# Where tiles start in SBUF: small tiles first, chunks and weight buffers 32 bytes further apart

## The chip, the core and the metric

The kernel runs on one core of a Trainium2 chip. Its engines are TensorE (PE: matmuls, and PEld: the load of the stationary operand), VectorE (DVE), ScalarE (ACT), GpSimd (POOL) and SyncE (SP, which issues most DMAs). They work from SBUF, a memory of 128 partitions; TensorE writes its sums into PSUM. The metric is the device time of one execution in microseconds (us); lower is better.

## What is computed

The reference is an encoder of two layers on 512 positions with 1024 features, all in float32. Each layer has a mixer and an MLP, with RMS norms in front and a last norm behind.

```python
for layer in range(DEPTH):                       # DEPTH = 2
    h = rms_norm(x, norm_mix[layer])
    if layer % N_MIXERS == 0:
        y = stick_breaking_attention(h, sb_w_qkv[ia], sb_w_o[ia])   # 16 heads of 64
    else:
        y = rglru_block(h, rg_w_in[ib], ..., rg_w_o[ib])            # gated linear recurrence, width 1024
    x = x + y
    h = rms_norm(x, norm_mlp[layer])
    x = x + squared_relu_mlp(h, mlp_w1[layer], mlp_w2[layer])       # relu(h @ w1)**2 @ w2, width 4096
return rms_norm(x, norm_final)
```

## The kernel before

**Split products.** Every large product is done with operands in two parts, a rounded high part (`float32r`) and the rest: `xgh` and `xgl` for the normed activations, `wh` and `wl` for the weights. `three` (lines 217 to 221) makes one product of a 128x128 block of weights with 512 columns of activations out of three matmuls: `wh` with the high activations (L219), `wl` with the high ones (L220), `wh` with the low ones (L221). The first operand of a matmul after the sum is the stationary one, which is loaded by an instruction of its own; the other, the moving one, is streamed through.

**Layout of activations.** `xgh`, `xgl`, `bh` and `bl` are tiles of 128 partitions by 8 chunks by 512 columns of 4 bytes: a chunk is 2048 bytes in each partition. `xgh` and `xgl` hold the normed input of a product; `bh` and `bl` the input of an output projection or, in the MLP, a part of the activations behind relu and square.

**Weights.** A slab of 1024x128 weights is fetched into a `raw` buffer, ScalarE copies it rounded into `wh`, and VectorE subtracts to get `wl` (`slab_parts`, `slab`, `operand`, `weights_high`). The pool `wpool` has four buffers of each; in the recurrent mixer a second pool, `wmore`, has two more. A slab is 4096 bytes in each partition.

**The MLP** uses a scheme of seven products of half-size blocks in place of eight. Its up projection (`up`, L965) has matmuls of 256 moving columns: slices of `xgh` and `xgl`, or of sums of them (`s41`, `low`, and a chunk of `bh` and `bl`), against slices of `wh` and `wl`. Its down projection (`times`, L1060) has the activations as the stationary operand (`bh` and `bl` for one half, `sh` and `sl` for the other) and 512 columns of `wh` or `wl` as the moving one. The value product of the attention (L475 to L477) has `xgh` and `xgl` as the stationary operand and 256 columns of weights as the moving one.

**Order and pools.** TensorE's order is the program's; the other engines are scheduled by the framework, in parts by hand. Pools take SBUF one behind the other in the order in which they are made, and a pool lays out its tiles by their names in the order in which they first occur; each tile is rounded up to 32 bytes. Tiles of 4 to 32 bytes (`eps_t`, the eight `lam_` tiles, `rt`, `rc`, `rp`, `rn`, `rr`) stand between the large ones. Pools that are closed leave their place to the next: the attention's tiles, the MLP's blocks and the recurrent mixer's tiles use the same bytes one after the other.

Of the kernel before, what the change touches and what calls it, by code (L numbers as in the profile page):

```python
# [61 lines left out]
def hybrid_encoder(  # L62
# [23 lines left out]
    nc = tc.nc  # L86
    V, A, G, PE = nc.vector, nc.scalar, nc.gpsimd, nc.tensor

    const = ctx.enter_context(tc.tile_pool(name="const", bufs=1))
    wpool = ctx.enter_context(tc.tile_pool(name="wpool", bufs=4))  # L90
    work = ctx.enter_context(tc.tile_pool(name="work", bufs=2))
# [22 lines left out]
    V.memset(ones, 1.0)  # L114
    ident = const.tile([P, P], F32, tag="ident", name="ident")
    make_identity(nc, ident)
    eps_t = const.tile([P, 1], F32, tag="eps", name="eps_t")
    V.memset(eps_t, EPS)

    xgh = const.tile([P, C, S], F32R, tag="xgh", name="xgh")  # L120
    xgl = const.tile([P, C, S], F32R, tag="xgl", name="xgl")
    bh = const.tile([P, C, S], F32R, tag="bh", name="bh")
    bl = const.tile([P, C, S], F32R, tag="bl", name="bl")

# [16 lines left out]
    class Squares:  # L141
# [21 lines left out]
        def inv_squares(self, ps):  # L163

            for t in range(S // P):
                PE.matmul(
                    ps[:, t : t + 1], self.acc[:, t * P : (t + 1) * P], ones[:, 0:1],
                    start=True, stop=True,
                )
            n = S // P  # L170
            rr = work.tile([P, 2 * n], F32, tag="rr", name="rr", bufs=1)
            V.tensor_scalar(rr[:, :n], ps[:, :n], 1.0 / D, EPS, ALU.mult, ALU.add)
            V.reciprocal(rr[:, :n], rr[:, :n])
            V.tensor_scalar(rr[:, n:], rr[:, :n], -1.0, None, ALU.mult)
            return rr


    def slab_parts(src, cuts):

        raw = wpool.tile([P, C, P], F32, tag="raw", name="raw", bufs=3)  # L180
        wh = wpool.tile([P, C, P], F32R, tag="wh", name="wh")
        wl = wpool.tile([P, C, P], F32R, tag="wl", name="wl")

        def fetch(i, queue=nc.sync):
            k = slice(*cuts[i : i + 2])
            queue.dma_start(out=raw[:, k, :], in_=src[:, k, :])

        def part(i, high=A.copy):
            k = slice(*cuts[i : i + 2])
            if high:  # L190
                high(wh[:, k, :], raw[:, k, :])
            if high == V.tensor_copy:
                return
            V.tensor_tensor(wl[:, k, :], raw[:, k, :], f(wh[:, k, :]), ALU.subtract)

        return wh, wl, fetch, part
# [5 lines left out]
    def slab(src, cut=1, ks=range(C)):  # L202
        raws = rawpools[next(loads) % len(rawpools)]
        raw = raws.tile([P, C, P], F32, tag="raw", name="raw", bufs=3 if raws is wpool else 1)
        k = slice(ks.start, ks.stop)
        nc.sync.dma_start(out=raw[:, k, :], in_=src[:, k, :])
        pool = wpools[next(slabs) % len(wpools)]
        wh = pool.tile([P, C, P], F32R, tag="wh", name="wh")
        wl = pool.tile([P, C, P], F32R, tag="wl", name="wl")
        for i in range(cut):  # L210
            k = slice(ks.start + i * len(ks) // cut, ks.start + (i + 1) * len(ks) // cut)
            A.copy(wh[:, k, :], raw[:, k, :])  # L212
            with tc.issue_after(behind[0]) if behind[0] else nullcontext():
                V.tensor_tensor(wl[:, k, :], raw[:, k, :], f(wh[:, k, :]), ALU.subtract)  # L214
        return wh, wl
# [15 lines left out]
    def beside(ws, ah, al, pss, at, ks=range(C)):  # L231
# [9 lines left out]


    lams = {
        n: const.tile([P, C], F32, tag=f"lam_{n}", name=n)
        for n in ("ab", "pp", "den", "s1", "s2", "pl", "c8", "c4")
    }
    c8, c4 = lams["c8"], lams["c4"]
# [42 lines left out]
    with ExitStack() as actx:  # L290
# [8 lines left out]
            fill=1.0, base=0, channel_multiplier=1,  # L299
        )  # L300

        scans = []
        for i in range(3):
            sc = sp.tile([P, S + 1], F32, tag=f"scan{i}", name=f"scan{i}")
            G.memset(sc[:, S : S + 1], 1.0)
            scans.append(sc)

        lasts = []
        for i in range(2):
            both = []  # L310
            for nm in ("h", "l"):
                t = sp.tile([P, 2 * P], F32R, tag=f"last{nm}{i}", name=f"last{nm}{i}")
                G.memset(f(t[:, :P]), 0.0)
                both.append(t)
            lasts.append(both)

        q, kh, kl, v, w = {}, {}, {}, {}, {}
        norm = {}
# [74 lines left out]
        others = {getattr(mybir.EngineType, e) for e in ("Activation", "DVE", "Pool", "SP")}  # L393
        with tc.manual_schedule(engines=others):
            A.dma_start(out=colt, in_=cols)
            A.activation(work.tile([P, 1], F32, tag="rt", name="early"), eps_t, AF.Sqrt)
            for j in range(2):
                parts[j][2](1, A)
            for c in range(C):
                nc.sync.dma_start(out=xcs[c], in_=xT[:, c, :])  # L400
                if c in (0, 3, 5):
                    for j in range(2):
                        parts[j][2]((c + 1) // 2)
            for j in range(2, 6):
                for i in range(2):
                    parts[j][2](i)

            parts[0][3](0, V.tensor_copy)
            for kind, c in START:
                if kind == "x":  # L410
                    halves("mix0", c, xcs[c])
                elif (kind, c) == ("q", 0):
                    parts[0][3](c, None)
                elif kind != "s":
                    parts["qknm".index(kind)][3](c)
                else:
                    A.activation(sqs[c], xcs[c], AF.Square)
                    if c:
                        V.tensor_tensor(sums, sums, sqs[c], ALU.add)

            for k in range(C):
                for n, (low, y) in enumerate(((0, xgh), (0, xgl), (1, xgh))):
                    for i in range(2):
                        PE.matmul(
                            first[i], parts[i][low][:, k, :], y[:, k, :], start=k == n == 0,
                            stop=k == C - 1 and n == 2,
                        )
            first_halves(*first)

        def inverse():  # L430

            pc = bank("z")
            for t in range(NB):
                PE.matmul(
                    pc[:, t : t + 1], sums[:, t * P : (t + 1) * P], ones[:, 0:1],
                    start=True, stop=True,
                )
            rc, rp, rn = (work.tile([P, NB], F32, tag=n, name=n, bufs=1) for n in ("rc", "rp", "rn"))
            diag = work.tile([P, S], F32, tag="sq", name="diag")
            with tc.high_priority():  # L440
                norm["root"] = A.activation(rc, pc[:, :NB], AF.Sqrt, bias=eps_t, scale=1.0 / D)
                V.reciprocal(rc, rc)
                for t in range(NB):
                    ts = slice(t * P, (t + 1) * P)
                    V.tensor_scalar(diag[:, ts], ident, rc[:, t : t + 1], None, ALU.mult)
                V.tensor_scalar(rp, rc, SCALE, None, ALU.mult)
                V.tensor_scalar(rn, rc, -SCALE, None, ALU.mult)
            norm.update(rc=rc, rp=rp, rn=rn)
            yield
            pr = bank("z")  # L450
            PE.matmul(pr, ones, diag, start=True, stop=True)
            r = work.tile([P, S], F32, tag="r", name="r")
            with tc.high_priority():
                norm["copy"] = A.copy(r, pr)
            norm["r"] = r
            yield
# [307 lines left out]
    class Mlp:  # L764
# [254 lines left out]

        def operand(self, raw):  # L1020
            pool = wpools[next(slabs) % len(wpools)]
            wh = pool.tile([P, C, P], F32R, tag="wh", name="wh")
            wl = pool.tile([P, C, P], F32R, tag="wl", name="wl")
            wh, wl = (t.rearrange("p (j k) f -> p j (k f)", j=2) for t in (wh, wl))
            self.A.copy(wh, raw)
            self.V.tensor_tensor(wl, raw, f(wh), ALU.subtract)
            return wh, wl
# [350 lines left out]
    with ExitStack() as rctx:  # L1378
# [48 lines left out]

        def weights_high(key):
            pool = wmore if next(made) % 6 > 3 else wpool
            wh = pool.tile([P, C, P], F32R, tag="wh", name="wh")  # L1430
            wl = pool.tile([P, C, P], F32R, tag="wl", name="wl")
            ws[key] = wh, wl
            OA.copy(wh, raws[key])

# [150 lines left out]
    with ExitStack() as mctx:  # L1585
# [27 lines left out]

        A.activation(lp.tile([P, 1], F32, tag="rt", name="early"), eps_t, AF.Sqrt)

        ss = lp.tile([P, NB, 3], F32, tag="ss", name="ss")
        bias = lp.tile([P, NB], F32, tag="bias", name="bias")

        def square(t, h, i, cols=slice(0, S), end=False):
# [17 lines left out]
            EG.tensor_tensor(y, y, gb[h][:, cols], ALU.mult)  # L1637

        def root(t, i):
            rt = work.tile([P, 1], F32, tag="rt", name="rt")  # L1640
            A.activation(rt, ss[:, t, i : i + 1], AF.Sqrt, bias=bias[:, t : t + 1], scale=1.0 / D)
            V.reciprocal(rt, rt)
            return rt
# [130 lines left out]
```

## Time and profile before

| | |
|---|---|
| median of 2 runs | 1043.64 us (1043.36 to 1043.92) |
| span of the profiled execution | 1041.3 us |
| TensorE's granted clock, mean | 0.999 |
| HBM read, written | 137.41 MB, 4.19 MB |

The profile is one execution. A busy time is the sum of an engine's instruction durations without overlap counted twice. Matmuls are pipelined: one starts long before the one ahead of it is recorded as ended, so the time between two starts is shorter than a duration. The chain of waits is the work that ended last, followed back from the end; it shows stretches of instructions with their count.

### The profile page before, as it was taken

The page shows a single profiled execution, that of the slowest core. Times are in us where ns is not written, and L with a number is a line of the kernel's source. Part 1 is how long each engine was busy: PE and PEld are TensorE (multiplying, and loading weights), DVE is VectorE, ACT ScalarE, POOL GpSimd, SP SyncE. Part 2 cuts the span into 40 slices and gives each one's busy share as a digit, 9 for nine tenths or more (in the row PEclk, how much of TensorE's full clock was granted, in tenths as well). Part 3 has the DMA queues.
Part 4 walks back from the last instruction along what each step waited for, and adds up shares of the span by engine and source line. Part 5 has one row for each costly group of instructions (what it writes and reads, how often), then busy time and mean ns, then how long its engine had stood idle before and what let it go on. Part 6 is the DMA issues. An engine that isn't in the chain of part 4 may idle for free.

```text
span 1041.3 us, 15858 instructions
## 1 busy us (share of the span) xinstructions
PE 1032.1 (99%) x5862; PEld 902.2 (87%) x5862; DVE 858.7 (82%) x1148; ACT 702.3 (67%) x1083; POOL 171.8 (17%) x239
## 2 busy tenths in 40 slices
PE   9999999999999999999999999999999999999997
PEld 7988888888888988988988888888888988988986
DVE  7888787848788898898899888984789797897897
ACT  6777676826766773773775799964755773773865
POOL 0444444420010010010011121200000010010012
PEclk9999999999999999999999999999999999999999
DMA  7745454528546667567682675453346667667663
GB/s 243 216 111 143 117 151 102 162 88 297 137 81 189 182 137 211 161 136 209 162 209 76 159 176 142 102 222 101 82 87 173 180 138 206 161 137 200 145 129 107
DMA packets 53260, 160.46 MB, mean 154 GB/s; under 512 B 6720, under 2 KB 8256, under 8 KB 53184
## 3 DMA queue, kind: packets, MB, share of 16 engines
q1 hardware_dynamic: 42096, 120.35, 35.5%
q0 software_dynamic: 10656, 38.80, 22.5%
q8 instruction: 46, 0.75, 0.3%
q10 hardware_dynamic: 432, 0.31, 0.1%
q14 instruction: 30, 0.25, 0.1%
HBM read 137.41 MB, written 4.19 MB: 136 GB/s over the span
## 4 chain that ended last, share of the span: by engine, by line
PE 96%; ACT 2%; DMA 1%; DVE 1%; issue 0%; POOL 0%; ACTq 0%; DVEq 0%
PE ps_t L1060 17%; PE ps_acc L965 10%; PE ps_acc L1060 8%; PE ps_z L965 8%; PE ps_acc L221 5%; PE ps_acc L219 5%; PE ps_acc L220 5%; PE ps_o L965 5%; PE ps_z L1060 4%; PE ps_t L219 2%; PE ps_t L220 2%; PE ps_t L221 2%; PE ps_o L219 2%; PE ps_o L220 2%; PE ps_o L221 2%; PE ps_z L221 2%
## 5 line engine op out<-in xcount | busy, mean ns | idle before, releaser
L754 ACT CAST wh<-b 128x1024 fp32r<-128x1024 f32 x168 | 174.1, 1047 | 126.1 <-DVE b L754 71.5
L754 DVE TENSOR_TENSOR wl<-b,wh 128x1024 fp32r<-128x1024 f32 x168 | 203.5, 1220 | 48.4 <-ACT wh L754 47.9
L1042 POOL DMA_DIRECT2D b<-in_w_dn x40 | 35.0, 874 | 364.3 <-DVE b L754 204.4
L219 PE MATMUL ps_acc<-xgh,wh 128*128 128x512 f32 x192 | 78.5, 409 | 0.0
L221 PE MATMUL ps_acc<-xgl,wh 128*128 128x512 f32 x192 | 75.2, 391 | 0.0
L220 PE MATMUL ps_acc<-xgh,wl 128*128 128x512 f32 x192 | 75.1, 391 | 0.0
L578 DVE TENSOR_TENSOR_SCAN scan<-keep,later 128x128 f32<-128x128 f32 (+1 forms) x64 | 59.9, 939 | 16.9 <-ACT keep L568 9.8
L214 DVE TENSOR_TENSOR wl<-raw,wh 128x512 fp32r<-128x512 f32 (+2 forms) x70 | 61.5, 906 | 14.9 <-ACT wh L212 14.8
L754 ACT ACTIVATE u<-u 128x512 f32<-128x512 f32 x100 | 63.1, 632 | 5.5 <-DVE u L754 3.8
L212 ACT CAST wh<-raw 128x512 fp32r<-128x512 f32 (+2 forms) x70 | 50.6, 758 | 20.6 <-PE ps_acc L221 7.3
L582 POOL TENSOR_TENSOR w<-w,scan 128x128 f32<-128x128 f32 (+1 forms) x64 | 51.9, 812 | 56.7 <-DVE scan L578 53.3
L1042 POOL DMA_DIRECT2D b<-in_w_up x24 | 20.8, 868 | 240.2 <-DVE b L754 71.8
L754 DVE TENSOR_TENSOR b<-b,b 128x1024 f32<-128x1024 f32 x48 | 58.7, 1222 | 1.3
L754 DVE TENSOR_TENSOR u<-u 128x512 f32<-128x512 f32 (+1 forms) x92 | 54.8, 596 | 2.7 <-ACT u L754 1.1
L965 PE MATMUL ps_z<-xgh,wh 128*128 128x256 f32 x192 | 54.2, 282 | 0.0
L965 PE MATMUL ps_z<-xgh,wl 128*128 128x256 f32 x192 | 54.1, 282 | 0.0
L754 ACT CAST wh<-raw 128x1024 fp32r<-128x1024 f32 x46 | 48.0, 1047 | 8.7 <-PE ps_acc L1060 6.7
L965 PE MATMUL ps_acc<-low,wh 128*128 128x256 f32 x192 | 53.9, 281 | 0.0
L1060 PE MATMUL ps_t<-wl,sh 128*128 128x512 f32 x126 | 50.1, 398 | 0.0
L1060 PE MATMUL ps_t<-wh,sh 128*128 128x512 f32 x126 | 49.7, 395 | 0.0
L1060 PE MATMUL ps_t<-wh,sl 128*128 128x512 f32 x126 | 49.5, 393 | 0.0
L1060 PE MATMUL ps_t<-wh,bh 128*128 128x512 f32 x126 | 49.3, 391 | 0.0
(399 smaller groups left out, 3420.7 us busy)
## 6 DMA issues: line engine op xcount, KB each, us to landing
b<-in_w_dn SPq DMA_DIRECT2D x48, 512.0 KB, 4.4
b<-in_w_dn POOLq DMA_DIRECT2D x40, 512.0 KB, 5.7
b<-in_w_up SPq DMA_DIRECT2D x36, 512.0 KB, 4.5
b<-in_w_up POOLq DMA_DIRECT2D x24, 512.0 KB, 5.5
raw<-in_w_m SPq DMA_DIRECT2D x16, 512.0 KB, 4.5
raw<-in_w_dn SPq DMA_DIRECT2D x16, 512.0 KB, 4.7
raw<-in_w_in SPq DMA_DIRECT2D x16, 512.0 KB, 3.8
raw<-in_w_qk SPq DMA_DIRECT2D x12, 512.0 KB, 3.7
```

The source lines that it names most:

```text
L212: A.copy(wh[:, k, :], raw[:, k, :])
L214: V.tensor_tensor(wl[:, k, :], raw[:, k, :], f(wh[:, k, :]), ALU.subtract)
L219: PE.matmul(ps, wh, ah, start=start, stop=False)
L220: PE.matmul(ps, wl, ah, start=False, stop=False)
L221: PE.matmul(ps, wh, al, start=False, stop=stop)
L578: V.tensor_tensor_scan(sc[:, S - n : S][:, ::-1], keep[:, :n][:, ::-1], later[:, S - n :][:, ::-1], 1.0, ALU.mult, ALU.max,)
L582: G.tensor_tensor(wt, wt, sc[:, S - n + 1 : S + 1], ALU.mult)
L754: ins = getattr(self.e, name)(*args, **kwargs)
L965: PE.matmul(ps[:, i * HS : (i + 1) * HS], m, y, start=new and i == k == n == 0, stop=i == 1 and k == C // 2 - 1 and n == 2, skip_group_che ...
L1042: G.dma_start(out=unit[b].rearrange("p j n -> p (j n)"), in_=unit["src"](to), accum_op=ALU.add)
L1060: PE.matmul(ps, m, y[:, jj, cols], start=first and n == 0, stop=last and n == 2, skip_group_check=not new,)
```

## The change

The tiles keep their shapes for all that uses them, and no product, copy or DMA is added, removed or resized. Five things differ:

- A pool `small` is made ahead of all others and takes the small tiles; `eps_t` is widened to 16 columns there.
- `xgh` and `xgl` get 8 more columns (32 bytes) behind each chunk of 512, so chunks are 2080 bytes apart.
- Each `wh` and `wl` buffer gets 8 more columns at its end (`half_slab`), so buffers are 4128 bytes apart.
- The three `scan` tiles of the attention, each of 513 columns, are made behind the `last` tiles and not ahead of them.
- `ss` is made flat and seen as 4 x 3 columns; its size stays.

```diff
+    small = ctx.enter_context(tc.tile_pool(name="small", bufs=1))
     const = ctx.enter_context(tc.tile_pool(name="const", bufs=1))
...
-    eps_t = const.tile([P, 1], F32, tag="eps", name="eps_t")
+    eps_t = small.tile([P, 16], F32, tag="eps", name="eps_t")[:, :1]
...
-    xgh = const.tile([P, C, S], F32R, tag="xgh", name="xgh")
-    xgl = const.tile([P, C, S], F32R, tag="xgl", name="xgl")
+    PAD = 8
+    xgh = const.tile([P, C, S + PAD], F32R, tag="xgh", name="xgh")[:, :, :S]
+    xgl = const.tile([P, C, S + PAD], F32R, tag="xgl", name="xgl")[:, :, :S]
...
-            rr = work.tile([P, 2 * n], F32, tag="rr", name="rr", bufs=1)
+            rr = small.tile([P, 2 * n], F32, tag="rr", name="rr")
...
+    def half_slab(pool, tag):
+        t = pool.tile([P, C * P + PAD], F32R, tag=tag, name=tag)
+        return t[:, : C * P].rearrange("p (c f) -> p c f", c=C)
...
-        wh = wpool.tile([P, C, P], F32R, tag="wh", name="wh")
-        wl = wpool.tile([P, C, P], F32R, tag="wl", name="wl")
+        wh = half_slab(wpool, "wh")
+        wl = half_slab(wpool, "wl")
...
-        n: const.tile([P, C], F32, tag=f"lam_{n}", name=n)
+        n: small.tile([P, C], F32, tag=f"lam_{n}", name=n)
...
-        scans = []
-        for i in range(3):
-            sc = sp.tile([P, S + 1], F32, tag=f"scan{i}", name=f"scan{i}")
-            G.memset(sc[:, S : S + 1], 1.0)
-            scans.append(sc)
-
         lasts = []
...
+
+        scans = []
+        for i in range(3):
+            sc = sp.tile([P, S + 1], F32, tag=f"scan{i}", name=f"scan{i}")
+            G.memset(sc[:, S : S + 1], 1.0)
+            scans.append(sc)
...
-            rc, rp, rn = (work.tile([P, NB], F32, tag=n, name=n, bufs=1) for n in ("rc", "rp", "rn"))
+            rc, rp, rn = (small.tile([P, NB], F32, tag=n, name=n) for n in ("rc", "rp", "rn"))
...
-            rt = work.tile([P, 1], F32, tag="rt", name="rt")
+            rt = small.tile([P, 1], F32, tag="rt", name="rt", bufs=2)
```

`slab`, `operand` and `weights_high` get the same edit as `slab_parts`, and the tile `early` at the kernel's start moves to `small` with `rt`. What comes of it is a table of starts. The "offset" is a tile's first byte in its partition divided by 32, modulo 8 (worked out from the sizes and the pools' order):

| tile | first byte before | offset before | first byte after | offset after |
|---|---|---|---|---|
| `xgh`, chunk c | 2592 + 2048 c | 1 for every c | 3072 + 2080 c | c |
| `xgl`, chunk c | 18976 + 2048 c | 1 for every c | 19712 + 2080 c | c |
| `bh`, `bl`, every chunk | 35360, 51744 | 1 | 36352, 52736 | 0 |
| `wh` of `wpool`, buffer i | 80672 + 4096 i | 1 for every i | 81408 + 4128 i | i |
| `wl` of `wpool`, buffer i | 97056 + 4096 i | 1 for every i | 97920 + 4128 i | 4 + i |
| `wh`, `wl` of `wmore` | from 144352 | 7 | from 145152 | 0, 1 and 2, 3 |
| MLP of layer 0: `s41`, `sh`, `sl` | from 166880 | 7 | from 167680 | 0 |
| MLP of layer 1: `s41`, `sh`, `sl` | from 167040 | 4 | from 167840 | 5 |
| tiles of `home` (`x`, seven of the `low`) | from 123872 | 7 | from 124672 | 0 |
| attention: `q`, `kh`, `kl`, `th`, `tl`, `v` | from 146400 | 7 | from 147200 | 0 |

Slices of 128 or 256 columns, 512 or 1024 bytes, have the offset of their tile or chunk.

On every engine but GpSimd the instructions stand in the same order as before. At GpSimd's start, ahead of all other work, these rows stand before (`ident` is the identity matrix for transposes, `later` the mask of the attention's scan, `lasth` and `lastl` its tiles for the last block of keys):

```order
masks.py:197 MEMSET ident 128x128
L296 MEMSET later 128x512
L305 MEMSET scan_105 128x1
masks.py:199 ISA
masks.py:199 AFFINE_SELECT ident<-ident 128x128
L305 MEMSET scan_107 128x1
L305 MEMSET scan_109 128x1
L313 MEMSET lasth_111 128x128
L313 MEMSET lastl_113 128x128
L313 MEMSET lasth_115 128x128
L313 MEMSET lastl_117 128x128
L297 AFFINE_SELECT later<-later 128x128
```

And these in the changed kernel, whose lines are numbered anew:

```order
masks.py:197 MEMSET ident 128x128
L302 MEMSET later 128x512
L313 MEMSET lasth_108 128x128
masks.py:199 ISA
masks.py:199 AFFINE_SELECT ident<-ident 128x128
L313 MEMSET lastl_110 128x128
L313 MEMSET lasth_112 128x128
L313 MEMSET lastl_114 128x128
L320 MEMSET scan_116 128x1
L320 MEMSET scan_118 128x1
L320 MEMSET scan_120 128x1
L303 AFFINE_SELECT later<-later 128x128
```

A memset of a `lasth` tile, of 128 columns, now stands ahead of the select on `ident` in place of one of a single column, and the three `scan` memsets come behind the four `last` ones.

More of the change, by code (lines that the diff above doesn't have):

```diff
@@ L207, in slab @@
         pool = wpools[next(slabs) % len(wpools)]
-        wh = pool.tile([P, C, P], F32R, tag="wh", name="wh")
-        wl = pool.tile([P, C, P], F32R, tag="wl", name="wl")
+        wh = half_slab(pool, "wh")
+        wl = half_slab(pool, "wl")
         for i in range(cut):
@@ L395, in hybrid_encoder @@
             A.dma_start(out=colt, in_=cols)
-            A.activation(work.tile([P, 1], F32, tag="rt", name="early"), eps_t, AF.Sqrt)
+            A.activation(small.tile([P, 1], F32, tag="rt", name="early", bufs=2), eps_t, AF.Sqrt)
             for j in range(2):
@@ L1021, in operand @@
             pool = wpools[next(slabs) % len(wpools)]
-            wh = pool.tile([P, C, P], F32R, tag="wh", name="wh")
-            wl = pool.tile([P, C, P], F32R, tag="wl", name="wl")
+            wh = half_slab(pool, "wh")
+            wl = half_slab(pool, "wl")
             wh, wl = (t.rearrange("p (j k) f -> p j (k f)", j=2) for t in (wh, wl))
@@ L1429, in weights_high @@
             pool = wmore if next(made) % 6 > 3 else wpool
-            wh = pool.tile([P, C, P], F32R, tag="wh", name="wh")
-            wl = pool.tile([P, C, P], F32R, tag="wl", name="wl")
+            wh = half_slab(pool, "wh")
+            wl = half_slab(pool, "wl")
             ws[key] = wh, wl
@@ L1614, in hybrid_encoder @@
         A.activation(lp.tile([P, 1], F32, tag="rt", name="early"), eps_t, AF.Sqrt)
-        ss = lp.tile([P, NB, 3], F32, tag="ss", name="ss")
+        ss = lp.tile([P, 3 * NB], F32, tag="ss", name="ss")[:, : 3 * NB]
+        ss = ss.rearrange("p (t i) -> p t i", t=NB)
         bias = lp.tile([P, NB], F32, tag="bias", name="bias")
```

## The prediction

> **What bounds the kernel now.** I read the page's busy shares and its summary of the chain of waits first.
>
> ```profile
> span 1041.3 us, 15858 instructions
> PE 1032.1 (99%) x5862; PEld 902.2 (87%) x5862; DVE 858.7 (82%) x1148; ACT 702.3 (67%) x1083; POOL 171.8 (17%) x239
> PE 96%; ACT 2%; DMA 1%; DVE 1%; issue 0%; POOL 0%; ACTq 0%; DVEq 0%
> ```
>
> TensorE is the chain for 96% of the span. Its instructions are fixed, so the only question is how far one matmul's start stands from the next one's, the step. The durations of single matmuls (391 ns for 512 columns) overlap and do not give it; the chain of waits does, since a piece of it with a count is that many matmuls in line. I asked for the chain around the first down projection of layer 0, then around the same stretch of layer 1 (start us, length us, what, count).
>
> ```profile
> 291.89 2.72 PE ps_t L1060 x12
> ...
> 297.33 2.75 PE ps_t L1060 x12
> ...
> 305.84 5.47 PE ps_t L1060 x24
> 311.30 5.47 PE ps_acc L1060 x24
> 316.77 5.47 PE ps_t L1060 x24
> ...
> 324.98 5.47 PE ps_t L1060 x24
> ```
>
> ```profile
> 761.40 2.72 PE ps_acc L1060 x12
> 764.12 2.81 PE ps_t L1060 x12
> ...
> 772.73 5.52 PE ps_t L1060 x24
> 778.25 5.57 PE ps_acc L1060 x24
> 783.82 5.54 PE ps_t L1060 x24
> ...
> 792.16 5.55 PE ps_t L1060 x24
> ```
>
> These are the same instructions on the same sizes; only addresses differ. I call "offset" a tile's start in units of 32 bytes, modulo 8 (the table in the section on the change). The 2.72 rows read the moving weights at offset 1 and the stationary `bh`, `bl` at offset 1: 2.72/12 = 226.7 ns a step. The 2.75 row has `sh`, `sl` of layer 0, at offset 7: 229.2 ns. The 2.81 row has them where layer 1 puts them, at offset 4: 234.2 ns. So the layout already costs 3% between one place and another, which is the effect that the change plays with. The matmuls of 256 columns show it too.
>
> ```profile
> 428.10 2.88 PE ps_z L965 x24
> 430.98 2.74 PE ps_o L965 x24
> ...
> 436.55 2.72 PE ps_o L965 x24
> ```
>
> ```profile
> 827.13 2.84 PE ps_o L965 x24
> 829.97 2.84 PE ps_z L965 x24
> 832.81 2.86 PE ps_o L965 x24
> ```
>
> At 428.10 the moving chunks of `xgh`, `xgl` and the weights are all at offset 1: 2.88/24 = 120.0 ns. At 436.55 the moving `s41` and `low` are at 7 and the weights at 1: 113.3 ns. In layer 1 the same product (832.81), with `s41` at 4 and some `low` at 7, takes 119.2 ns. Equal offsets are thus the best row for 512 columns and the worst for 256.
>
> **The change part by part.** No engine gets another instruction, another size or another wait; only GpSimd's few opening memsets change places. What changes is that today's relations (moving minus stationary offset: almost always 0) become all eight. The chunks of `xgh` and `xgl` run through offsets 0 to 7, the four `wh` of the main pool stand at 0 to 3 and the four `wl` at 4 to 7, `bh` and `bl` at 0. So I price a mixture, in four terms, by the step count of each line.
>
> ```profile
> 0.00:1041.30 1041.30, 199.46 (x496) 1.00 0.58 154
> 0.00:1041.30 1041.30, 311.16 (x1356) 1.00 0.58 154
> 0.00:1041.30 1041.30, 239.53 (x2016) 1.00 0.58 154
> 0.00:1041.30 1041.30, 36.88 (x128) 1.00 0.58 154
> 0.00:1041.30 1041.30, 12.92 (x48) 1.00 0.58 154
> ```
>
> From the windows view of the whole span, one line of code each: L219 (L220 and L221 have as many), L1060, L965, L475 (L476 and L477 as many), L424. What L219 to L221 take today stands in the timeline of TensorE in a stretch without waits, and in the count of the window over it.
>
> ```profile
> 241.81 0.39 PE L219 MATMUL ps_acc<-bh,wh 128*128 128x512 f32 x1
> ...
> 266.75 0.39 PE L221 MATMUL ps_t<-xgl,wh 128*128 128x512 f32 x1
> 242.00:266.90 24.90, 24.90 (x111) 1.00 0.94 336
> ```
>
> 111 matmuls have 110 steps: 24.94/110 = 226.7 ns.
>
> A mixture of offsets, 512 columns: 0 apart 226.7, two apart (1 and 7 are two from each other modulo 8) 229.2, three apart 234.2; the relation one apart has no row. I bound it by the best and the worst, 226.7 and 234.2, and take 230, their middle. That distances of 3 and 5, or 0 and 4, cost alike is an assumption: no row has them apart. The mean of the four is 230.0. 256 columns: 120.0, 113.3 and 119.2; the fourth lies between 113.3 and 120.0, taken as 117.5. The mean is 117.5.
>
> Term 1, L219 to L221 and L424, 3 x 496 + 48 = 1536 steps. Today 226.7, and where the weights lie in the second pool (offset 7) 229.2; I take 227.5. To 230.0: +2.5 ns, +3.8 us. Bounds: -0.8 ns (-1.2 us) to +6.7 ns (+10.3 us).
>
> Term 2, L1060, 1332 steps of 512 columns (the 24 of the last half-width products are left out). Today 5.47/24 = 227.9 in layer 0 and 5.545/24 = 231.0 in layer 1, mean 229.5. To 230.0: +0.7 us. Bounds: -2.8 ns (-3.7 us) to +4.7 ns (+6.3 us).
>
> Term 3, L965, 2016 steps. Today's longest pieces of the chain:
>
> ```profile
> 330.45 13.98 PE ps_acc L965 x120
> ...
> 797.72 14.26 PE ps_acc L965 x120
> ```
>
> That is 116.5 and 118.8 ns; with the single products above, at 113.3 to 120.0, I take 118.1. To 117.5: -1.2 us. Bounds: -4.8 ns (-9.7 us) to +1.9 ns (+3.8 us). The products with `s41` lose their good relation of layer 0, those with `xgh` leave the worst one.
>
> Term 4, L475 to L477, 384 steps, all offsets equal today, so 120.0. To 117.5: -1.0 us. Bounds: -2.6 to 0.
>
> Sum: 3.8 + 0.7 - 1.2 - 1.0 = +2.3 us. Ends: all at the best rows -17.2 us, all at the worst +20.4 us.
>
> The other engines read and write at moved addresses as well. The one row that shows the same operation on buffers at different offsets is VectorE's subtraction, whose sources stand at 7 in layer 0 and at 4 in layer 1 (min, median, max in ns).
>
> ```profile
> L754 DVE TENSOR_TENSOR wl<-b,wh x168: 1170/1219/1228, 270.8 to 1026.2; 128x1024 fp32r<-128x1024 f32 x168
> ```
>
> Its largest stands 9 ns above its median, so I price these at nothing; if they cost 1%, DVE's 82% busy share would take it in, except in the 1% of the chain that is DVE. GpSimd's select on `ident` slides by one memset of the same kind, and `scan` gets its ones later; `ident` is first read long after.
>
> ```profile
> 1.56 0.29 POOL masks.py:199 TENSOR_SCALAR_AFFINE_SELECT ident<-ident 128x128 f32<-128x128 f32 x1
> ...
> L600 PE MATMUL ps_t<-ident,w x160: 270/272/327, 50.3 to 228.5; 128*128 128x128 f32 x160
> ```
>
> It is there 48 us before its first use: nothing, and without that cover it would be 0.1 us.
>
> The profiled execution has a span of 1041.3 us against a median of 1043.6, so 2.3 us lie around it; with +2.3 the forecast is 1045.9, or **1046 us**.
>
> A rule that speaks against the whole sum: the rows 2.72 and 2.81 show that stationary and moving reads are not indifferent to each other's place. The Trainium skill's page "TensorE: Matmul & The Clock Gate", Part 2, says the opposite: TensorE has two independent read ports, and loading the next weights takes no read bandwidth from the running matmul. By it the sum would be 0; the trace disagrees with it by 7.5 ns in 227. The same page's Part 1 puts the step of a warm 512-column bf16 matmul at 215.7 ns; if a layout could free that much here, the estimate from it would be 11 ns x 2868 = 32 us less, and no run here shows it.
>
> **The rivals.**
> A. *Half of the starts gain from alignment.* Today the moving operand of each 512-column step of L219 to L221 and L1060 starts at an odd offset, 32 bytes past a multiple of 64; afterwards half of them start on one. The two rows 120.0 and 113.3 show that a step can lose 6.7 ns whole. If every even start saves that: 2868/2 x 6.7 = -9.6 us, and half of the 2400 steps of 256 columns come to 113.3, 4.8 below today: -5.8 us. Together -15.4, so 1028 us; if all steps got it, 1013. For it: nothing in the trace has such a start at 512 columns. Against it: `s41` at offset 4 (119.2) is no better than at 7.
> B. *Slower: no pattern comes to rest.* The rows 226.7 repeat for 110 steps on end because every step has the same offsets. If a new offset with every chunk throws each step onto the worst relation, 512 columns take 234.2 and 256 columns 119.2: +10.3 + 6.3 + 2.2 - 0.3 = +18.5 us, so 1062. It decides for the other side of 2% once the unknown relation exceeds 234.2 by about another nanosecond on average (2.5 us / 2868). For it: layer 1's rows at offset 4 never settle to 226.7. Against: layer 0 at offset 7 is only 1% above 226.7.
> C. *Nothing.* The change doesn't do what it is made for, as gains and losses cancel or reads are independent: 1043.6.
>
> **How the numbers follow.** Mixture 0.52 (1040 to 1053 by itself), A 0.20, B 0.16, C 0.12. The range reaches to 1026 and 1062, which leaves out the far half of A and the far part of B, some 0.17. Faster by over 2% (below 1022.8, about what a measurement of this kernel can tell from no change): the part of A in which more than half of the steps gain, 0.12. Slower by over 2% (above 1064.5): the upper part of B, 0.10. Within: 0.78.
>
> **What would show it.** In the new trace the 110-step stretch of L219 to L221 should take about 25.3 us (230 ns) in place of 24.94; A says 24.6 or less, B 25.7. The x120 pieces of L965 should come to about 14.1 us in both layers, with no more 2.88 beside 2.72; the x24 pieces of L1060 at 5.44 to 5.62 according to the weight buffer. A steady 220 ns in any piece of 512 columns would make the forecast wrong by alignment; pieces of over 5.65 would make it wrong by B. If ACT or DVE rises above a few per cent of the chain, my price of nothing for them is wrong.

## The result and the profile after

| | before | after |
|---|---|---|
| median | 1043.64 us (2 runs, 1043.36 to 1043.92) | 1050.34 us (2 runs, 1049.65 to 1051.03) |
| span of the profiled execution | 1041.3 us | 1049.2 us |
| TensorE's granted clock, mean | 0.999 | 0.999 |

The ratio is 1.0069, with a 95% interval from 1.0052 to 1.0085: slower by 6.7 us in the medians and by 7.9 us between the two profiled spans. All ratios in this text leave out two of the eleven executions of `sums_two_apart` below, which took 1719.8 us (at a granted clock of 0.557) and 2085.4 us. The page of the changed kernel (its lines of code are numbered 6 higher) answers to the three lines shown of before:

```profile
span 1049.2 us, 15858 instructions
...
PE 1040.2 (99%) x5862; PEld 903.3 (86%) x5862; DVE 859.1 (82%) x1148; ACT 702.6 (67%) x1083; POOL 170.9 (16%) x239
...
PE 93%; DVE 3%; ACT 1%; issue 1%; DMA 1%; ACTq 0%; POOL 0%; DVEq 0%; POOLq 0%
```

The instruction counts are the same, and the busy times of DVE, ACT and POOL within 1 us; TensorE alone is busy 8 us longer. So its steps became longer. The chain of waits shows where (start us, length us, what, count); first layer 0, the down projection and then the up projection:

```profile
308.20 5.60 PE ps_t L1066 x24
313.79 5.51 PE ps_acc L1066 x24
319.30 5.60 PE ps_t L1066 x24
...
333.21 14.13 PE ps_acc L971 x120
```

```profile
425.88 2.86 PE ps_z L971 x24
428.75 2.86 PE ps_acc L971 x24
431.60 2.83 PE ps_z L971 x24
```

And layer 1:

```profile
939.08 5.51 PE ps_t L1066 x24
944.60 5.58 PE ps_acc L1066 x24
950.18 5.51 PE ps_t L1066 x24
...
964.04 14.22 PE ps_acc L971 x120
```

Where layer 0 had 5.47 and layer 1 some 5.54, both now lie between 5.51 and 5.60 (229.6 to 233.3 ns a step), and which one depends on the piece, not on the layer. In the up projection no 2.88 stands beside a 2.74 any more. The dense products lost most in sum. In TensorE's timeline, the first and the last matmul of the stretch whose 110 steps took 24.94 us before, and the window over it:

```profile
243.07 0.40 PE L225 MATMUL ps_acc<-bh,wh 128*128 128x512 f32 x1
...
268.54 0.39 PE L227 MATMUL ps_t<-xgl,wh 128*128 128x512 f32 x1
```

```profile
243.25:268.70 25.45, 25.45 (x111) 1.00 0.90 329
```

25.47/110 = 231.5 ns, where 226.7 stood.

**The steps of every kernel in one table.** The table gives mean steps in ns, from one matmul's start to the next one's over the whole trace of a kernel's profiled execution. It leaves out steps that a wait held up (steps of over 248 ns at 512 columns and of over 141 ns at 256). "dense" is L219 to L221 and L424 of before; "down" are the 512-column steps of L1060, "up" is L965, both by layer (0, 1); "value" is L475 to L477.

| kernel | dense | down, `bh` `bl` (0, 1) | down, `sh` `sl` (0, 1) | up (0, 1) | value |
|---|---|---|---|---|---|
| before | 228.3 | 227.1, 228.1 | 229.1, 233.9 | 117.4, 118.9 | 119.0 |
| after | 232.0 | 231.5, 231.9 | 231.7, 231.1 | 118.0, 118.6 | 118.2 |
| no_pads | 228.2 | 227.0, 229.9 | 226.7, 233.2 | 120.0, 119.2 | 119.1 |
| pads_on_activations | 231.5 | 227.2, 229.9 | 227.0, 233.2 | 118.6, 117.9 | 118.5 |
| pads_on_weights | 232.1 | 231.5, 231.4 | 231.9, 231.0 | 117.2, 118.1 | 118.2 |
| four_apart | 232.3 | 232.8, 233.0 | 228.9, 233.3 | 119.5, 118.2 | 118.9 |
| second_layer_level | 228.3 | 227.0, 227.0 | 226.7, 226.9 | 120.0, 120.0 | 119.1 |
| up_two_apart | 228.2 | 227.0, 229.9 | 226.9, 233.3 | 117.8, 115.7 | 119.2 |
| level_and_two_apart | 228.2 | 227.0, 227.2 | 226.9, 227.1 | 117.8, 117.2 | 119.2 |
| before_second_layer | 228.3 | 227.0, 227.1 | 229.1, 229.1 | 117.4, 117.6 | 119.0 |
| both_layers_level | 228.3 | 227.1, 227.2 | 227.1, 227.0 | 117.4, 117.6 | 119.0 |
| sums_two_apart_again | 228.1 | 227.0, 227.1 | 227.0, 227.1 | 117.4, 117.6 | 119.0 |

Below, the "relation" of a matmul is the offset of its stationary operand less that of its moving one, modulo 8. The prediction counted it the other way round and treated both signs alike.

### The profile page after: what moved, and what is told of

It is laid out like the page before. It is cut to its first block, busy times and chain, and to the rows that moved or that the text cites. A ratio compares the mean times of both kernels' runs of the same rounds, so it can differ in the third digit from the quotient of the medians.

```text
span 1049.2 us, 15858 instructions
## 1 busy us (share of the span) xinstructions
PE 1040.2 (99%) x5862; PEld 903.3 (86%) x5862; DVE 859.1 (82%) x1148; ACT 702.6 (67%) x1083; POOL 170.9 (16%) x239
## 4 chain that ended last, share of the span: by engine, by line
PE 93%; DVE 3%; ACT 1%; issue 1%; DMA 1%; ACTq 0%; POOL 0%; DVEq 0%; POOLq 0%
PE ps_t L1066 15%; PE ps_acc L971 8%; PE ps_z L971 8%; PE ps_acc L1066 7%; PE ps_acc L225 5%; PE ps_acc L226 5%; PE ps_acc L227 5%; PE ps_o L971 5%; PE ps_z L1066 4%; PE ps_t L225 2%; PE ps_t L226 2%; PE ps_t L227 2%; PE ps_o L225 2%; PE ps_o L227 2%; PE ps_o L226 2%; PE ps_t L606 2%
## 5 line engine op out<-in xcount | busy, mean ns | idle before, releaser
L1066 PE MATMUL ps_t<-wl,bh 128*128 128x512 f32 x126 | 49.7, 394 | 0.0
```

The lines of the kernel that those rows point to most:

```text
L1066: PE.matmul(ps, m, y[:, jj, cols], start=first and n == 0, stop=last and n == 2, skip_group_check=not new,)
```

## The experiments

Each ratio below is to the kernel before, timed in the same round; its medians there were 1043.44, 1042.97, 1043.40 and 1043.14 us.

**steps_by_offset: the disputed price by itself.** This kernel leaves out the encoder. It has eight moving chunks (`a` to `h`, offsets 0 to 7) and eight stationary ones, and 48 matmuls in line on each of the 64 pairs, at 512 columns (groups `w_`) and at 256 (`h_`); behind them come groups in which the offset turns at every third matmul.

```diff
+    for n, size in ((S, "w"), (S // 2, "h")):
+        for m in range(C):
+            for s in range(C):
+                ps = group(f"{size}_{NAMES[m]}{NAMES[s]}", n, lambda k: (m, s))
...
+                ps[:, :n], still[:, s, k % C * P : (k % C + 1) * P], moving[:, m, :n],
```

> This kernel leaves out the whole encoder: it copies x and eight slabs of weights into tiles whose chunks start at offsets 0 to 7 (in 32 bytes, modulo 8) and runs 48 matmuls in line for each of the 64 pairs of a moving and a stationary offset, at 512 and at 256 columns, and then groups in which the offsets turn every third matmul. Theory R (the relation of the two offsets sets the step, modulo 4): 512 columns 226.7 ns wherever the offsets are equal, 229 two apart, 234 where the stationary one is three ahead; 256 columns 120.0 where equal and 113.3 two apart; and it does not matter whether an offset is even. Rival E (an even start saves a step of 6.7 ns): the rows of even moving offsets stand at 220 and 113.3 whatever the weights. Rival S (a pattern that stays the same comes to rest at a good step, one that turns does not): all 64 pairs of 512 columns near 226.7 to 229, and only the groups with turning offsets at 231 or more.

The chain of this kernel, the groups with the moving operand at offset 3 (`d`) and the stationary at 0 to 7, first of 512 and then of 256 columns:

```profile
282.82 11.20 PE w_da L52 x48
294.02 10.99 PE w_db L52 x48
305.01 11.19 PE w_dc L52 x48
316.20 10.89 PE w_dd L52 x48
327.09 11.19 PE w_de L52 x48
338.28 11.20 PE w_df L52 x48
349.48 11.23 PE w_dg L52 x48
360.72 11.16 PE w_dh L52 x48
...
919.95 5.76 PE h_da L52 x48
925.71 5.65 PE h_db L52 x48
931.37 5.65 PE h_dc L52 x48
937.02 5.76 PE h_dd L52 x48
942.78 5.68 PE h_de L52 x48
948.45 5.47 PE h_df L52 x48
953.92 5.76 PE h_dg L52 x48
959.68 5.69 PE h_dh L52 x48
```

A piece divided by 48 is the step: 226.9 ns where both stand at 3 (`w_dd`), 229.0 where the stationary stands two below (`w_db`), 232.5 to 234.0 everywhere else. The steps from the 20th on, over all 64 pairs, go by the relation alone, within 0.7 ns at 512 columns and with a few exceptions at 256; the commonest value of each:

| relation | 0 | 1 | 2 | 3 | 4 | 5 | 6 | 7 |
|---|---|---|---|---|---|---|---|---|
| 512 columns, ns | 226.7 | 233.4 | 233.4 | 234.4 | 232.4 | 233.3 | 228.9 | 233.3 |
| 256 columns, ns | 120.0 | 118.3 | 117.8 | 117.4 | 118.7 | 119.9 | 117.8 | 117.8 |

Three things follow. The count runs modulo 8, not 4: 4 apart costs 232.4, not 226.7. The sign matters: 6 costs 228.9 and 2 costs 233.4. Even or odd starts are no matter: `a` with `a` takes as long as `b` with `b`. The mean over the eight relations is 232.0 ns at 512 columns and 118.5 at 256. The groups that turn at every third matmul come to 230.3 to 232.6 and 117.3 to 119.1; relation 0 itself, when both operands turn, takes 230.3 and no longer 226.7.

**no_pads: the small tiles alone.** The change without its pads, so that nearly all relations are 0.

```diff
-    PAD = 8
+    PAD = 0
```

> The changed kernel with the eight extra columns taken away again, small tiles still in front: all offsets are equal (0) in the attention, the first MLP and the recurrent mixer, and 0 against 5 in part of the last MLP. Theory R: products of 512 columns back at 226.7 in the first layer (L219 to L221, L1060: together some 2 us better than the kernel before), products of 256 columns all at 120.0 there (2.8 us worse), the last MLP's relation unknown: 1041 to 1048 us, likeliest 1044.5. Rival E (even starts help): some 15 us better than before, 1028. Rival M (the move of the small tiles, not the extra columns, cost the time): 1050.

1044.1 us against 1043.44 for the kernel before: ratio 1.0009, interval 1.0000 to 1.0018. The dense steps are those of before. The move of the small tiles alone brings layer 0's `sh`, `sl` from relation 6 (229.1) to 0 (226.7), and its whole up projection to 120.0, where `s41` and `low` had relation 2 before and the mean was 117.4. One takes back the other, so the move alone isn't the loss.

In layer 1 the table of relations isn't the whole account. There `bh` and `bl` stand at relation 0 too and yet average 229.9. Their matmuls come mostly in runs of 12 behind runs of `sh`, `sl`, which are at relation 5 (233.2). The first eight steps of such a run average 231.0 and only the 9th to 11th are down to 226.7: a step depends on what ran before it as well, and a short run doesn't reach the steady value.

**pads_on_activations and pads_on_weights: each pad alone.**

```diff
 def half_slab(pool, tag):
-        t = pool.tile([P, C * P + PAD], F32R, tag=tag, name=tag)
+        t = pool.tile([P, C * P], F32R, tag=tag, name=tag)
```

> The extra columns behind each chunk of the normed activations alone; weight buffers 4096 bytes apart, all at offset 0. Theory R: L219 to L221 on xgh and xgl as in the changed kernel (about 231.7 ns, +4 us against before), L1060 as without extra columns: 1046 to 1050, likeliest 1048. If the weight buffers alone cost the time: that of no_pads.

```diff
-    xgh = const.tile([P, C, S + PAD], F32R, tag="xgh", name="xgh")[:, :, :S]
-    xgl = const.tile([P, C, S + PAD], F32R, tag="xgl", name="xgl")[:, :, :S]
+    xgh = const.tile([P, C, S], F32R, tag="xgh", name="xgh")[:, :, :S]
+    xgl = const.tile([P, C, S], F32R, tag="xgl", name="xgl")[:, :, :S]
```

> The extra columns in the weight buffers alone; xgh and xgl all at offset 0. Theory R: each product has one relation for the wh steps (buffer 0 to 3) and one for the wl steps (4 more, alike modulo 4), so the steps differ from product to product between 226.7 and 234 and average near 230: L1060 as in the changed kernel (+2 us), L219 to L221 +3 us: 1046 to 1050, likeliest 1048. If only chunks whose offset turns cost anything: that of no_pads.

Pads on the activations alone: 1047.04 us, ratio 1.0034 (1.0021 to 1.0046). Pads on the weights alone: 1049.45 us, 1.0058 (1.0042 to 1.0073). Added up on top of `no_pads`, the two would make 1.0083, which the interval of the whole (1.0052 to 1.0085) still holds. The steps show that they don't add up: either pad is enough to spread the dense products over the relations, with 231.5 and 232.1 ns there, and 232.0 with both. The down projection reads no `xgh`, so only the pads on the weights reach it (227 to 231.5 in layer 0).

**four_apart: a constant bad relation, without any turning.** This is `no_pads` with 128 bytes ahead of `xgh` and behind `bl`, so that the four tiles stand 4 offsets from all weights.

```diff
+    const.tile([P, 32], F32, tag="gap0", name="gap0")
     xgh = const.tile([P, C, S + PAD], F32R, tag="xgh", name="xgh")[:, :, :S]
...
     bl = const.tile([P, C, S], F32R, tag="bl", name="bl")
+    const.tile([P, 32], F32, tag="gap1", name="gap1")
```

> The kernel of no_pads (no columns between chunks or buffers, small tiles in front) with 128 bytes more ahead of xgh and after bl, so that the normed activations, bh and bl start four offsets (of 32 bytes, counted modulo 8) from every buffer of the weights, and nothing turns. Theory R8 (the step hangs on the stationary offset less the moving one modulo 8, as steps_by_offset gave it: 226.7 at 0, 232.4 at 4 for 512 columns; 120.0 and 118.7 for 256): the 1536 dense steps 226.9 to 232.4, +8.4 us; bh and bl in the down projection +2.7; the up projection's 1248 steps on xgh, xgl or bh/bl -1.6; the value product -0.5; in sum +9.0 on no_pads' 1044.1, so 1053. Theory R4 (the prediction's assumption that 0 and 4 apart cost alike): no change, 1044.

1052.8 us, ratio 1.009 (1.0076 to 1.0103), where R8 had 1053: at least as slow as the changed kernel with its pads. Its chain, in the down projection of layer 0, has 231 ns in every piece (`bh`, `bl` at 232.8, and behind them `sh`, `sl`, which are still at relation 0, at 228.9), where `no_pads` behind it has 5.44/24 = 226.7:

```profile
308.27 5.55 PE ps_t L1068 x24
313.83 5.55 PE ps_acc L1068 x24
319.38 5.55 PE ps_t L1068 x24
```

```profile
305.00 5.44 PE ps_t L1066 x24
310.44 5.44 PE ps_acc L1066 x24
315.88 5.44 PE ps_t L1066 x24
```

So a bad relation is enough to make a kernel this slow, without any change from chunk to chunk. Turning isn't free either (230.3 for 226.7 at relation 0 above), but the changed kernel needs no extra price for it: its dense steps, 232.0, are the mean over the relations.

**second_layer_level, up_two_apart, level_and_two_apart: the table put to use.** The first takes the last layer's small tiles (160 bytes, five offsets) out of the way by using tiles that exist. The second writes the up projection's weights 64 bytes further in, in buffers that hold `wh` and `wl` in one tile, for a relation of 2. The third does both.

```diff
-        lp = mctx.enter_context(tc.tile_pool(name="last", bufs=1))
...
-        bias = lp.tile([P, NB], F32, tag="bias", name="bias")
+        bias = lams["s1"][:, :NB]
```

> The kernel of no_pads, with the four small tiles of the last layer (160 bytes, which put that layer's pool five offsets off) kept in tiles that are there already, so that every tile that matmuls read starts at offset 0. Theory R8: in the second MLP the down projection's 333 steps on bh/bl go from 229.9 to 226.7 and its 333 on sh/sl from 233.2 to 226.7, -3.2 us; the up projection's 384 steps on s41 or low from 117.4 to 120.0, +1.0; 1044.1 to 1041.8. If the slower steps of that layer come from something other than its offset (its place in memory, the work beside it), they stay: 1044.

```diff
+            t = pool.tile([P, n], F32R, tag=f"pair{i}", name=f"pair{i}", bufs=1)
+            t = [t[:, j * C * P + shift : (j + 1) * C * P + shift] for j in range(2)]
...
-                ws[i] = made[i] = self.operand(self.source(unit(i), name))
+                ws[i] = made[i] = self.operand(
+                    self.source(unit(i), name), 16 if steps[i][0] == "up" else 0
+                )
```

> The kernel of no_pads, with the weights' buffers 64 bytes longer, and the up projection's weights written 64 bytes further in, so that they (stationary) start two offsets behind the activations (moving), while every 512-column product keeps offset 0 to 0. Second MLP's pool still five offsets off. Theory R8: the up projection's 1632 steps with a relation of 2 go from 120.0 to one of the two steps that steps_by_offset showed there, 117.8 or 113.3: -3.6 to -10.9 us, 1033 to 1040.5; its 384 steps on the second MLP's s41 and low near 119.9. If the step is set elsewhere (a wait for the weights' copies takes the place of the step): 1044.

> Both edits together: every 512-column product at a relation of 0, the up projection at 2 in both MLPs. Theory R8: the down projection's 1332 steps all at 226.7 (-3.2 us on no_pads), the up projection's 2016 steps from 119.9 to between 113.3 and 117.8 (-4.4 to -13.3): 1027.6 to 1036.5, faster than both kernels. If the two gains aren't independent, or a wait takes their place, it stays above 1038.

The steps came out as the table says, the time did not. `second_layer_level` brought all 512-column steps to 226.7 to 228.3, and the times are 1044.15 us, ratio 1.0011 (1.0002 to 1.0020), against 1.0009 for `no_pads`. In its profiled execution the steps are 2.1 us shorter than those of `no_pads` (down 2.9 less, up 0.8 more), the start at L424 1.6 us longer and the held-up steps of the MLPs 0.7; whether the start is longer in every execution one trace can't tell.

The edit also did something besides levelling the layer. Ahead of the last layer a small activation named `early` makes ACT load the table for the square roots at the end. With its tile in the pool `small`, the framework schedules it at the kernel's start, and the load falls among the last layer's work. `no_pads`, then `second_layer_level`:

```profile
684.61 1.28 ACT L1620 ACT_TABLE_LOAD   x1
```

```profile
2.65 0.19 ACT L1619 ACTIVATE early<-eps_t 128x1 f32<-128x1 f32 x1
...
1028.00 1.28 ACT L1649 ACT_TABLE_LOAD   x1
```

From the start of the last matmul to the end of the span it is 7.5 us there, and 6.6 in `no_pads`: another 1.0 us. `level_and_two_apart` and `sums_two_apart_again` (below) have the late load too, and 7.4 us; all the others lie at 6.6 to 6.7. No run moves the load alone, so that it is the cause is not shown. With it the account of the profiled span closes: -2.1 + 1.6 + 0.7 + 1.0 = +1.2, measured +1.1.

`up_two_apart` cut the up projection from 120.0 and 119.2 to 117.8 and 115.7, both values of relation 2 occurring in it. In the second layer's stretch the chain shows 2.72/24 = 113.3:

```profile
972.50 2.72 PE ps_z L978 x24
975.22 2.72 PE ps_acc L978 x24
977.94 2.72 PE ps_z L978 x24
```

And yet it takes 1044.61 us, ratio 1.0018 (1.0009 to 1.0027); `level_and_two_apart` takes 1044.44 us, 1.0011 (1.0002 to 1.0020). The waits view of `up_two_apart` has a first row that `no_pads` lacks, and another, further down, that is 0.4 us there (engine, waited for: us in total, times, longest):

```profile
PE ps_acc L233 <- DVE pair L227: 2.3, 3, 1.0
...
PE ps_z L978 <- ACT u L767: 1.1, 1, 1.1
```

Summed over all held-up steps of `up_two_apart`, dense products lose 3.4 us more than in `no_pads`, L424's stretch at the start 0.7, the down projection 1.5 and the up projection 1.1. That is 6.7 us against 2013 x (119.6 - 116.7) = 5.8 us gained, and the time from the first to the last matmul moved by +1.0. Of the 3.4 us, 2.8 are three waits in the attention, before 195 us, and the first matmul of L978, the up projection, starts at 333 us. So these come from the other half of the edit, the common tile, which changes the order on DVE and ACT in the attention from 86 us on, and not from shorter steps. The 2.6 us in the MLP may come from either; that was not separated. `level_and_two_apart` has the same account: 7.1 us of shorter steps against `no_pads`, 6.9 us of longer waits, and the longer end besides.

**before_second_layer, sums_two_apart, both_layers_level: the table on the kernel before.** In the first and the third only starts change, and every engine keeps its order; the second builds on `second_layer_level` and has its late table load. The first widens one tile of 48 bytes, so that the second MLP lies at offset 7, as the first does.

```diff
-        ss = lp.tile([P, NB, 3], F32, tag="ss", name="ss")
+        ss = lp.tile([P, NB, 10], F32, tag="ss", name="ss")
```

> The kernel before, with one tile of the last layer's pool 112 bytes longer (it takes 96 more with its rounding), so that the second MLP's pool starts at offset 7 like the first's, where it was at 4. Theory R8: the second MLP's steps become those of the first: the down projection on sh/sl from 233.9 to 229.1 and on bh/bl from 228.1 to 227.1, the up projection on s41 from 117.8 to 113.8 and on low from 119.5 to 115.6: -1.9 and -1.5 us, 1040.1 beside 1043.5 for the kernel before, ratio 0.9967. If the second MLP's steps hang on something else than its offset: 1043.5.

1040.93 us (11 runs) against 1043.40 for the kernel before (22 runs): ratio 0.9976, interval 0.9968 to 0.9985. The second layer's steps became the first's, as forecast: 229.1 for 233.9 on `sh`, `sl`, and 117.6 for 118.9 in the up projection. Of the 3.4 us expected 2.5 came: in the trace the steps are 3.2 us shorter and the held-up ones of the MLPs 0.7 longer.

`sums_two_apart` starts from `second_layer_level` and puts `s41` and the low halves two offsets below everything else; `both_layers_level` comes to the same relations in both MLPs from `before_second_layer`, with 64 bytes behind `s41`.

```diff
-            self.s41 = self.bp.tile([P, C // 2, S], F32R, tag="s41", name="s41", bufs=1)
+            t = self.bp.tile([P, C // 2 * S + 16], F32R, tag="s41", name="s41", bufs=1)
+            self.s41 = t[:, : C // 2 * S].rearrange("p (c s) -> p c s", s=S)
```

> The kernel of second_layer_level with six small tiles moved between the work tiles and the home tiles, and 64 bytes more behind s41: the weights (all buffers), xgh, xgl, bh, bl, sh and sl start at one offset, and s41 and the low halves two offsets below it, in both MLPs, so that the up projection's 768 steps on them have a relation of 2 and every 512-column product one of 0. Theory R8: the down projection's 1332 steps near 226.9 (-3.9 us on the kernel before); the up projection's steps on s41 and low between 113.3 and 117.8 in both MLPs, where the kernel before has 113.8 and 115.6 in the first and 117.8 and 119.5 in the second (+1.3 to -1.9 us), and on xgh, xgl, bh, bl at 120.0 against 119.2 (+1.0 us); in sum -1.6 to -4.8 us against the kernel before, 1039 to 1042 beside a kernel before at 1043.5. If steps that become shorter are taken back by waits, as in the two kernels with the shifted weights: no change.

> The kernel of before_second_layer with 64 bytes more behind s41, so that sh and sl start at the weights' offset 1 in both MLPs (relation 0), while s41 and the low halves stay two offsets below it. Theory R8: the down projection's 666 steps on sh/sl from 229.1 to 226.9, -1.5 us; nothing else moves: 1039.4 beside a kernel before at 1043.4, ratio 0.9962. If the floor is elsewhere by now (sums_two_apart, with the same relations, was timed at 0.9973): 1040.6.

> The kernel of sums_two_apart once more, for a profile at the full clock. Theory R8, by the relations: the down projection near 226.9 in both MLPs, the up projection's steps on s41 113.8 to 114.2 and on low 115.6 to 116.0, on xgh 119.1 to 120.0; span 1037 to 1040.

`sums_two_apart`: 1040.8 us, ratio 0.9973 (0.9964 to 0.9982); the steps in the table are those of a second run of it, `sums_two_apart_again` (1041.39 us, span 1039.6). `both_layers_level`: 1040.91 us, ratio 0.9979 (0.9970 to 0.9988), with the steps forecast, in layer 1 too:

```profile
934.16 5.44 PE ps_acc L1061 x24
939.60 5.44 PE ps_t L1061 x24
...
953.20 13.98 PE ps_acc L966 x120
...
975.80 2.74 PE ps_o L966 x24
```

All three beat both kernels, by 2.2 to 2.6 us against before. But the last 1.5 us, `sh` and `sl` from 229.1 to 227.1, don't show against `before_second_layer`: 1039.4 was expected of `both_layers_level`. The waits of the weight load say where a small part of it goes: before, then in `before_second_layer`, then in `both_layers_level`:

```profile
PEld ps_t L1060 <- DVE wl L754: 1.2, 4, 0.3
```

```profile
PEld ps_t L1060 <- DVE wl L754: 2.0, 6, 0.6
```

```profile
PEld ps_t L1061 <- DVE wl L754: 2.3, 6, 0.6
...
PEld ps_acc L966 <- ACT u L754: 0.6, 1, 0.6
```

The low halves of the weights come from DVE at their own pace; a TensorE that is ahead of them waits. Most of that wait came with `before_second_layer`; the last edit adds 0.3 us to it. Against before, the steps of `both_layers_level` are shorter by 4.6 us (up 1.4, down 3.2), its held-up steps in the MLPs longer by 1.2, and L424's start, which differs by up to 2 us between these traces, was 0.7 shorter: 4.1 in sum, and by that the time from first to last matmul fell in that execution.

That execution was the fastest of the eleven (1039.17 us); in the medians 2.2 us are left. `sums_two_apart_again` has the same steps to 0.2 ns and took 1041.39 us: in its trace L424's start is 1.1 us longer, the up projection's waits 0.6 and the end behind the last matmul 0.7. So the start and the waits move a single execution by more than the 1.5 us looked for. How they lie in most executions stays open; one trace of each kernel can't tell.

## Why the prediction was right in direction and short in size

The bound and the mechanism stood: TensorE's steps set the time, the change spreads the relations, and the layout that is taken away was close to the best for 512 columns. The forecast was 1046 us, the time is 1050.3, inside the range; but the sum of +2.3 us was a third of what came. Term by term, with steps from the table above:

| term | steps | today, taken / measured | after, forecast / measured | forecast | measured |
|---|---|---|---|---|---|
| 1, dense | 1536 | 227.5 / 228.3 | 230.0 / 232.0 | +3.8 us | +5.7 us |
| 2, down | 1332 | 229.5 / 229.6 | 230.0 / 231.6 | +0.7 | +2.7 |
| 3, up | 2016 | 118.1 / 118.2 | 117.5 / 118.3 | -1.2 | +0.2 |
| 4, value | 384 | 120.0 / 119.0 | 117.5 / 118.2 | -1.0 | -0.3 |
| sum | | | | +2.3 | +8.3 |

Held-up steps and the start change by less than 1 us together, and the profiled span grew by 7.9 us.

- *The step that failed* is the price of the mixture: "The mean of the four is 230.0", and for 256 columns 117.5. It rested on the assumption "that distances of 3 and 5, or 0 and 4, cost alike", and on "one apart" lying midway. `steps_by_offset` has 232.4 at 4 and 233.3 to 233.4 at one apart. The row of 229.2, moving 1 and stationary 7, is relation 6, and was taken for relation 2 too, which costs 233.4. With all eight the mean is 232.0, and that is what the dense products take (232.0) and nearly what the down projection takes (231.6); by the starts, each relation has between 160 and 250 of the 1536 dense matmuls, so the spread is nearly even. `four_apart` shows the same in the whole kernel: by the assumption 1044, by the table 1053, measured 1052.8.
- *Term 3*: the 113.3 row was taken for a quarter of the mixture. Relation 2 takes 113.3 in two groups of eight and 117.8 in the other six, and the mean over all relations is 118.5.
- *Term 4* took all steps of today at 120.0; they were at 119.0.
- *Today's relations* were read as "almost always 0". By the table of starts they are so for the value product and most dense products, but not for 666 of the 1332 steps of the down projection and 768 of the 2016 of the up projection. The terms took those steps at their measured length, so no term hangs on it.
- *Rival A, alignment,* falls: no 512-column group at an even start is below 226.7, and the table of relations repeats from chunk to chunk whether starts are even or odd.
- *Rival B, nothing comes to rest,* is off in its price, 234.2 for every step, but it was nearer to the mechanism than the 230.0: the 226.7 steps are gone from the dense products, and seven of the eight relations lie from 228.9 to 234.4.
- *Rival C* falls with the interval of the ratio. By the Trainium skill's page "TensorE: Matmul & The Clock Gate", Part 2, loading the next weights takes no read bandwidth from the running matmul; by that rule alone the 64 groups would be alike, and they differ by 7.7 ns in 227.
- *Price of nothing for the other engines:* it stands. DVE's busy time went from 858.7 to 859.1 us. DVE's 3% of the chain, 1% before, isn't a new wait: steps held up in the MLPs came to about 1 us less.
- *The signs named ahead:* the 110-step stretch took 25.47 us (25.3 forecast, 25.7 by B); the x120 pieces 14.13 and 14.22 (about 14.1); the x24 pieces of the down projection lay between 5.51 and 5.60 (5.44 to 5.62); no steady 220 came.

## What to carry to other kernels

Where TensorE sets the time and a stationary operand is loaded for every matmul, note each operand's first byte modulo 256 and keep stationary and moving tiles of 512-column float32r products equal in it; a pool of small tiles ahead of large ones can undo that for everything behind it, as 160 bytes did here in one layer (`before_second_layer`, 0.9976). Don't spread starts to be safe: an even spread costs the mean over all relations (232.0 against 226.7). And a price for a mixture needs a row for each of its members, signs too; a kernel with one group of matmuls for each settles it in one run. What such a kernel gives are steady values: runs of 12 matmuls behind a bad relation stay above them (229.9 for 226.7 in `no_pads`).

## What was not expected of the hardware

- From the 20th step on, a step depends on stationary less moving start in units of 32 bytes, modulo 8, over all 64 pairs: 226.7 to 234.4 ns at 512 columns, 113.3 to 120.0 at 256. The best relation of 512 columns, 0, is the worst of 256.
- At 256 columns one relation can have two steady steps: relation 2 at 117.8 in six groups and 113.3 in two, each time with 120.0 in the group behind it (`h_df` and `h_dg`), where relation 3 has 117.4 otherwise. What decides between them stays open.
- The steady values 113.3, 120.0 and 226.7 are 17, 18 and 34 times 6.67 ns, the difference of the first two, while the other relations turn between several values. That suggests something that recurs every 6.67 ns; it was not tried.
- TensorE's gains didn't all reach the time: 4.6 us of shorter steps in `both_layers_level` left 2.2 us in the medians.
